# Dilated attention, dilation 16: the scores of all eight blocks in one list, both halves' transposes in one list, and the statistics three products earlier

## The chip, the cores and the metric

The kernel runs on one core of a Trainium2 chip. The metric is the device time of one launch in microseconds (us). TensorE (PE) multiplies matrices and loads its weights beside (PEld), VectorE (DVE) and ScalarE (ACT) do elementwise work, GpSimd (POOL) does little here, and SyncE (SP) issues nearly all DMAs. Each engine works through its own queue in order, and waits there for semaphores.

## The reference

Two layers: dilated sliding-window attention and an MLP, then a gated linear recurrence (HGRN) and an MLP, each with a residual and a layer norm. The change is in the attention: three head groups with (window, dilation) = (128, 1), (512, 4) and (2048, 16), 16 heads of 64, 1024 positions. Cut to what matters:

```python
def dilated_attention_mixer(x, w_in, w_out):
    proj = (x @ w_in).reshape(B, S, N_GROUPS, 3, ATTN_HEADS, ATTN_HEAD_DIM)
    for g, (window, dilation) in enumerate(DILATED_PATTERNS):
        q = rotary(proj[:, :, g, 0], pos)
        k = rotary(proj[:, :, g, 1], pos)
        o, lse = dilated_window_attention(q, k, proj[:, :, g, 2], window, dilation)
        ...
    wts = jax.nn.softmax(jnp.stack(lses, axis=0), axis=0)
    o = jnp.einsum('gbsh,gbshe->bshe', wts, jnp.stack(outs, axis=0).astype(F32))
    return o.reshape(B, S, ATTN_HEADS * ATTN_HEAD_DIM).astype(x.dtype) @ w_out
```

Inside `dilated_window_attention` every position attends to itself and to those at distances d, 2d, ... behind it: p = exp(s - m), l = sum p, o = (p / l) v, lse = m + log l.

## The kernel before

The attention takes its heads in eight pairs (`pr`). A pair and a dilation form a unit; the units go in the order dilation 16, 4, 1 within a pair (`GORD`), two units to a group (`a` = 0 and 1), twelve groups `gi`. The dilation-16 units are `a` = 0 of groups 0, 3, 6, 9 and `a` = 1 of groups 1, 4, 7, 10.

Each group's projection is 21 products (`product`): seven block products of a Strassen-like scheme (`ORDA`) for three columns of blocks (q, k, v). A product is twelve 128x512 matmuls, L832 to L834, with a weight tile `H` whose high half ScalarE writes (L499) and whose low half VectorE writes (L507), and operands `xh` and `xl` that SyncE loads (L461). Three PSUM banks hold the products.

What else the attention does is hung between the products. `fill[n]` is the list that runs after product n, then `low_w(n + 3)` and `split_w_(n + 5)` follow. TensorE and VectorE keep the order in which the code is written (`in_order`); a scheduler places ScalarE's and SyncE's instructions. `unit_work` gives a unit's steps, and tables say at which product after `base` they run: `ROPES` (rotation of q and k, with loads `rot` by SyncE, L539, used at L542 and L543), `UNIT0` and `OFFS` (six lists of `pieces`), `STATS` (three steps) and `MIX`.

For dilation 16 the lists of `pieces` hold: the scores of four blocks (`qk16`, L607), each followed by reductions on VectorE (L610: masked minimum of the negated scores, into `sS`) and exponentials on ScalarE (L614, with their sums); the transposes of v (`vtrans`, L557); the transposes of p (`ptr16`, L623); and the value products (`pv16`, L635).

The three steps of `STATS` come from `combine_tr`: TensorE transposes the units' minima and sums (L726) and ScalarE evicts them (`sr`); ScalarE's queue stores them to memory (L732); SyncE loads them back in another layout (`ml`, L739, eight DMAs for dilation 16). `ml` is a tile with one buffer, made anew for each pair. When the three units of a pair are done, `combine` (steps of `MIX`) turns `ml` into weights `fh` and `fl` on VectorE (L754 to L773, the last read of `ml` is `fl`, L773), SyncE brings them to `frow` (L778), TensorE spreads them (`fb`, L790), and VectorE multiplies the units' outputs by them (L793 to L796). After the last group, what is left of `fill` and the lists of the last pair are woven into the out-projection (L204 to L206, weights `woh`, `wol`, activations `aoh`, `aol`).

Of the kernel before, what the change touches and what calls it, by code (L numbers as in the profile page):

```python
# [9 lines left out]
F32 = mybir.dt.float32  # L10
F32R = mybir.dt.float32r
U8 = mybir.dt.uint8
AF = mybir.ActivationFunctionType
ALU = mybir.AluOpType
AX = mybir.AxisListType

P = 128
# [3 lines left out]
HD = 64  # L21
NPAIR = 8
DIL = (1, 4, 16)
# [46 lines left out]
def trunk_kernel(  # L70
# [24 lines left out]
    nc = tc.nc  # L95
    cp = ctx.enter_context(tc.tile_pool(name="cp", bufs=1))
    up = ctx.enter_context(tc.tile_pool(name="up", bufs=NSLOT))
    wp = ctx.enter_context(tc.tile_pool(name="wp", bufs=3))
# [7 lines left out]
    def bank(tag, name):  # L106
        return ps.tile([P, 512], F32, name=name, tag=tag, bufs={"mm": 3, "s": 2, "pt": 2, "o": 1}[tag])
# [4 lines left out]
    act = nc.scalar.activation  # L112
# [250 lines left out]
    def attention(pre, hc):  # L363
        out_of = []

        def evict(*args, **kw):
            act(*args, **kw)
            out_of.append(latest())
# [4 lines left out]
        groups = [units[i:i + 2] for i in range(0, len(units), 2)]  # L373
# [72 lines left out]
        def get_T(m, n):  # L446
            if m >= 7 * len(groups):
                return
            i = ORDA[m % 7]
            if m >= 7 and m % 7 < RESIDENT:  # L450
                opT[m] = opT[m % 7]
                return
            if m < 7:
                if m not in opT:
                    opT[m] = make_T(i)
                return
            if m not in opT:
                opT[m] = [None, None]
            opT[m][n] = [U("xhl"[0] + "hl"[n], F32R) for _ in range(2)]
            for q in range(2):  # L460
                nc.sync.dma_start(opT[m][n][q].bitcast(F32), xtd[i - 1, n][:, q * 1024:(q + 1) * 1024])  # L461
# [3 lines left out]
        def load_w(n):  # L465
            if n >= len(seq):
                return
            gi, i, j = seq[n]
            for half in {1: (0,), 2: (0,), 6: (0, 1), 7: (0, 1), 3: (0, 1), 5: (1,), 4: (1,)}[i]:
                if (gi, j, half) not in raw:  # L470
                    raw[gi, j, half] = U("w" + "ab"[half])
                    nc.sync.dma_start(raw[gi, j, half], w_attn[pairs[gi][j][half]])
# [36 lines left out]
        mask = cp.tile([P, 384], F32, name="mask")  # L509
# [35 lines left out]
        def pieces(pr, g, qT, kT, vT, og, sS, tail):  # L545
            st = {}
# [48 lines left out]
                            act(p[h], p[h], AF.Exp, bias=sS[:, 0, h, b:b + 1], scale=-1.0,  # L595
                                accum_out=sS[:, 1, h, b:b + 1])

            def qk16(j):
                sb = [bank("s", "s") for _ in range(2)]
                whole = wp.tile([P, 512], F32, name="p", tag="p")  # L600
                blocks = [(b, cl, slice((b % 4 * 2 + cl) * 64, (b % 4 * 2 + cl) * 64 + 64))
                          for b in range(4 * j, 4 * j + 4) for cl in range(2)]
                for b, cl, c in blocks:
                    q = slice(b * P + cl * 64, b * P + cl * 64 + 64)
                    for h in range(2):
                        r = slice(h * HD, (h + 1) * HD)
                        nc.tensor.matmul(sb[cl][(h ^ cl) * HD:(h ^ cl) * HD + HD, b % 4 * 64:b % 4 * 64 + 64],  # L607
                                         qT[r, q], kT[r, q], start=True, stop=True, skip_group_check=True)
                for b, cl, c in blocks:
                    nc.vector.tensor_tensor_reduce(whole[:, c], sb[cl][:, b % 4 * 64:b % 4 * 64 + 64],  # L610
                                                   mask[:, 320:384], -0.125, 3.0e38, op0=ALU.add, op1=ALU.min,
                                                   accum_out=sS[:, 0, cl, b:b + 1])
                for b, cl, c in blocks:
                    act(whole[:, c], whole[:, c], AF.Exp, bias=sS[:, 0, cl, b:b + 1], scale=-1.0,  # L614
                        accum_out=sS[:, 1, cl, b:b + 1])
                st["p", j] = whole

            def ptr16(j):
                pt = bank("pt", "ppt")
# [7 lines left out]
            def pv16():  # L627
                o = [bank(tag, "o") for tag in ("o", "pt")]
                for b in range(8):
                    pts = st["pt", b // 4]  # L630
                    for cl in range(2):
                        r = slice(cl * 64, cl * 64 + 64)
                        for h in range(2):
                            m = b % 4 * P + (h ^ cl) * 64
                            nc.tensor.matmul(o[cl][h * HD:(h + 1) * HD, b * 64:b * 64 + 64],  # L635
                                             st["vn"][r, b * P + h * HD:b * P + (h + 1) * HD], pts[r, m:m + 64],
                                             start=True, stop=True, skip_group_check=True)
                for cl in range(2):
                    evict(og.rearrange("p (n b x) -> p x b n", b=8, x=2)[:, cl],
                        o[cl].rearrange("p (b n) -> p b n", b=8), AF.Copy)  # L640

# [52 lines left out]
            def run(f, bs):  # L694
                return [lambda b=b: f(b) for b in bs]
# [10 lines left out]
                ]  # L706
            first, second = [lambda: pv(0, 1, 2, 3)], [lambda: pv(4, 5, 6, 7)]
            if g == 2:
                return [run(qk16, (0,)) + [vtrans], run(qk16, (1,)) + run(ptr16, (0,)), run(ptr16, (1,)),
                        [pv16], [], []]  # L710
            if g == 1:
                return [qks((0, 2), (4, 6)) + [vtrans], [shift] + qks((1,), (3,)) + run(ptr, ((0, 2), (4, 6))),
                        qks((5,), (7,)) + run(ptr, ((1,), (3,))), first + run(ptr, ((5,), (7,))), [], second]
# [95 lines left out]
        def at(slot, f):  # L809
            fill.setdefault(slot, []).append(f)  # L810
# [119 lines left out]
        for n in range(len(seq)):  # L930
            gi, i, j = seq[n]
            load_w(n + LOADW)
            if j == 0 and n // 3 < 6:
                get_T(n // 3 + 1, 1)
            if j == 1 and n // 3 >= 5:
                get_T(n // 3 + 2, 0)
            if j == 2 and n // 3 >= 5:
                get_T(n // 3 + 2, 1)
            if n == 11:
                constants()  # L940
            if n == 30:
                constants2()
            if n == 36:
                hc.append(hgrn_consts())
            if n == len(seq) - 2 * PREA - 3:
                early = pre(oN)
            if n >= len(seq) - 2 * PREA - 1:
                next(early, None)
            if n == FIRSTO[0]:
                acts.__enter__()  # L950
            if n == FIRSTO[1]:
                acts.__exit__()
            if n in KEEP:
                keep_T(KEEP[n])
            product(n)
            for f in fill.pop(n, []):
                f()
            if n in FIRSTW:
                for f, m in FIRSTW[n]:
                    (split_w_, low_w, third_a, third_b, third_c, third_d)[f](m)  # L960
            else:
                low_w(n + SPLITW - 2)
                split_w_(n + SPLITW)
            if n % 21 == 14:
                last = gi == len(groups) - 1
                base = n + 7
                work = [unit_work(gi, a, base) for a in range(2)]
                for a in range(2):
                    adds, rope_of, core, stats, mix = work[a]
                    steps = [f for t in range(2) for f in (lambda rope_of=rope_of, t=t: rope_of(t),  # L970
                                                           lambda adds=adds, t=t: adds[t][0](),
                                                           lambda adds=adds, t=t: adds[t][1]())]
                    if last:
                        both = [lambda f=f: (f[0](), f[1]()) for f in (steps[1:3], steps[4:6])]
                        tail.append(([steps[0], both[0], steps[3], both[1]], core, stats, mix))
                        continue
                    for k, f in zip(ROPES[a], steps):
                        at(base + k, f)
                    for k, f in enumerate(core):
                        at(base + UNIT0 + OFFS[a][k], f)  # L980
                    for k, f in zip(STATS[a], stats):
                        at(base + k, f)
                    for k, f in zip(MIX[a], mix):
                        at(base + k, f)
                if last:
                    for a in range(2):
                        for k, f in list(zip(ROPES0[a], tail[a][0])):
                            if k < -1:
                                at(base + k, f)
                                tail[a][0].remove(f)  # L990
# [957 lines left out]
    pr = Out(w_attn_out, "a", 0)  # L1948
    hc = []
    oN, fill = attention(pr.pre_steps, hc)  # L1950
    gw = GateW()
    f = ffn(0, x1d, ln_ffn_g[0], ln_ffn_b[0], False, (gw.ask, lambda: gw.prefetch(0)))
# [6 lines left out]
    f = ffn(1, x5d, ln_ffn_g[1], ln_ffn_b[1], True)  # L1959
# [81 lines left out]
```

## Time and profile before

| what | us |
|---|---|
| median of 3 runs | 2724.91 (2723.44 to 2725.13) |
| the profiled execution | 2721.81 |
| its span, first to last instruction | 2720.0 |
| attention's units, first to last list | about 85 to 960 |
| out-projection beside the last units | from about 890 |

The granted TensorE clock of that execution was 0.999. Timeline rows give the start, the length, the engine, the line, the operation, the tile written and the tiles read, and the count; idle time before an instruction and what ended it stand in brackets. TensorE's starts tell more than its lengths, since matmuls overlap. Of dilation 16, TensorE's records count two to a matmul in the scores and the value products.

### The profile page before, as it was taken

What the parts mean: (1) busy time and instruction counts of PE and PEld (TensorE: products, weight loads), DVE (VectorE), ACT (ScalarE), POOL (GpSimd) and SP (SyncE); (2) the same over time, 40 slices, a digit from 0 to 9 for tenths busy, and PEclk for the clock granted to TensorE, in tenths of its full rate; (3) what the DMA queues carried; (4) which work ended last, traced back from release to release, by engine and by line L of the source; (5) the groups of instructions that cost most, each with busy time, mean ns of one, the idle gap of its engine ahead of it and who ended that gap; (6) DMA issues with size and microseconds to landing.
All of it is one profiled execution on the core that took longest, in us unless ns stands there. A gap on an engine that the chain in (4) does not pass through costs nothing.

```text
span 2720.0 us, 44143 instructions
## 1 busy us (share of the span) xinstructions
PE 2694.8 (99%) x16256; PEld 2199.3 (81%) x16256; DVE 2042.1 (75%) x3887; ACT 1385.0 (51%) x3044; POOL 39.2 (1%) x44
## 2 busy tenths in 40 slices
PE   9999999999999999999999999999999999999998
PEld 7787888888788677888888888788878888888887
DVE  8868877787887788876687686656478886678687
ACT  5555555555565455444544345555453544545443
POOL 0000000000000002000000000000000100000000
PEclk9999999999999999999999999999999999999999
DMA  8877666766767443554665652010233464485653
GB/s 303 269 226 226 219 217 203 246 216 220 251 208 245 126 137 140 200 187 151 229 238 189 206 170 93 32 63 32 74 128 116 150 225 161 154 305 174 224 178 124
DMA packets 208152, 493.66 MB, mean 181 GB/s; under 512 B 30016, under 2 KB 44864, under 8 KB 207936
## 3 DMA queue, kind: packets, MB, share of 16 engines
q1 hardware_dynamic: 204384, 481.14, 53.0%
q0 software_dynamic: 2304, 8.39, 0.8%
q8 instruction: 128, 2.10, 0.3%
q10 hardware_dynamic: 1248, 1.31, 0.2%
q14 instruction: 88, 0.72, 0.1%
HBM read 362.69 MB, written 94.11 MB: 168 GB/s over the span
## 4 chain that ended last, share of the span: by engine, by line
PE 92%; DVE 5%; ACT 1%; issue 1%; DMA 0%; POOL 0%; SPq 0%; DVEq 0%; ACTq 0%; POOLq 0%
PE pmm L834 7%; PE pmm L832 7%; PE pmm L833 7%; PE pup L1357 7%; PE pup L1355 7%; PE pup L1356 7%; PE pdy L1510 4%; PE pdy L1509 4%; PE pdy L1506 4%; PE pmm L192 3%; PE pdx L1509 3%; PE pdx L1510 3%; PE pdx L1506 3%; PE pmm L194 3%; PE pmm L193 3%; PE pmm L205 2%
## 5 line engine op out<-in xcount | busy, mean ns | idle before, releaser
L832 PE MATMUL pmm<-xh,H 128*128 128x512 f32 x1008 | 404.1, 401 | 1.4 <-ACT H L499 1.4
L834 PE MATMUL pmm<-xh,H 128*128 128x512 f32 x1008 | 395.6, 392 | 2.2 <-DVE H L507 2.1
L833 PE MATMUL pmm<-xl,H 128*128 128x512 f32 x1008 | 393.3, 390 | 0.7 <-DVE xl L158 0.7
L834 PEld LDWEIGHTS pmm<-xh,H 128*128 128x128 f32 x1008 | 189.5, 188 | 46.7 <-DVE H L507 5.4
L832 PEld LDWEIGHTS pmm<-xh,H 128*128 128x128 f32 x1008 | 189.9, 188 | 39.6 <-ACT H L499 2.2
L833 PEld LDWEIGHTS pmm<-xl,H 128*128 128x128 f32 x1008 | 190.1, 189 | 37.8 <-DVE xl L158 1.1
L1506 PE MATMUL pdy<-dT,dS 128*128 128x512 f32 x512 | 199.2, 389 | 0.0
L1509 PE MATMUL pdy<-dT,dS 128*128 128x512 f32 x512 | 199.2, 389 | 0.0
L1510 PE MATMUL pdy<-dT,dS 128*128 128x512 f32 x512 | 199.2, 389 | 0.0
L157 ACT ACTIVATE dS<-dr 128x512 fp32r<-128x512 f32 x192 | 119.3, 622 | 67.5 <-PE pdy L1510 36.1
L192 PE MATMUL pmm<-f0nh,wh 128*128 128x512 f32 x384 | 153.3, 399 | 0.0
L193 PE MATMUL pmm<-f0nl,wh 128*128 128x512 f32 x384 | 149.8, 390 | 0.0
L194 PE MATMUL pmm<-f0nh,wl 128*128 128x512 f32 x384 | 149.8, 390 | 0.0
L595 ACT ACTIVATE p<-p,stats 128x192 f32<-128x192 f32 (+1 forms) x256 | 108.8, 428 | 62.4 <-DVE stats L592 62.2
L158 DVE TENSOR_TENSOR dS<-dr,dS 128x512 fp32r<-128x512 f32 x192 | 131.4, 685 | 9.2 <-ACT dS L157 9.2
L157 ACT ACTIVATE dT<-hold 128x512 fp32r<-128x512 f32 x128 | 80.1, 626 | 80.8 <-DVE hold L1485 33.4
L1316 ACT ACTIVATE H<-wc 128x512 fp32r<-128x512 f32 x128 | 77.2, 625 | 76.6 <-DVE wc L1309 46.3
L1506 PEld LDWEIGHTS pdy<-dT,dS 128*128 128x128 f32 x512 | 96.1, 188 | 20.0
L1509 PEld LDWEIGHTS pdy<-dT,dS 128*128 128x128 f32 x512 | 96.1, 188 | 20.0
L1510 PEld LDWEIGHTS pdy<-dT,dS 128*128 128x128 f32 x512 | 96.1, 188 | 19.9
L592 DVE CUSTOM_DVE_ANT_0 p<-s,mask 128x192 f32<-128x192 f32 (+1 forms) x256 | 71.1, 337 | 45.3 <-PE s L579 32.4
L499 ACT ACTIVATE H<-wc 128x512 fp32r<-128x512 f32 x108 | 66.6, 629 | 75.6 <-DVE wc L491 73.5
(426 smaller groups left out, 6881.9 us busy)
## 6 DMA issues: line engine op xcount, KB each, us to landing
xh<-xtd SPq DMA_DIRECT2D x110, 512.0 KB
xl<-xtd SPq DMA_DIRECT2D x110, 512.0 KB
dr<-hd SPq DMA_DIRECT2D x192, 256.0 KB
dr<-in_w_down_dram SPq DMA_DIRECT2D x128, 256.0 KB
rot<-e SPq DMA_DIRECT2D x192, 128.0 KB
wa<-in_w_up_dram SPq DMA_DIRECT2D x48, 512.0 KB
wb<-in_w_attn_dram SPq DMA_DIRECT2D x36, 512.0 KB
wa<-in_w_attn_dram SPq DMA_DIRECT2D x33, 512.0 KB
```

Source lines behind the costliest of these rows:

```text
L157: act(hi, raw, AF.Copy)
L192: nc.tensor.matmul(o, wh[:, k], xs.h(k), start=k == 0, stop=False)
L193: nc.tensor.matmul(o, wh[:, k], xs.l(k), start=False, stop=False)
L194: nc.tensor.matmul(o, wl[:, k], xs.h(k), start=False, stop=k == NK - 1)
L832: nc.tensor.matmul(o, wh, hi[k // 2][:, c], start=begin and k == 0, stop=False, skip_group_check=True)
L833: nc.tensor.matmul(o, wh, lo[k // 2][:, c], start=False, stop=False, skip_group_check=True)
L834: nc.tensor.matmul(o, wl, hi[k // 2][:, c], start=False, stop=end and k == 3, skip_group_check=True)
L1355: nc.tensor.matmul(o, wh, xf.h(b, k), start=begin and k == 0, stop=False, skip_group_check=True)
L1356: nc.tensor.matmul(o, wh, xf.l(b, k), start=False, stop=False, skip_group_check=True)
L1506: nc.tensor.matmul(o[q], h, T_[:, L], start=begin, stop=False, skip_group_check=True)
L1509: nc.tensor.matmul(o[q], h, T_[:, R], start=False, stop=False, skip_group_check=True)
L1510: nc.tensor.matmul(o[q], l, T_[:, L], start=False, stop=end, skip_group_check=True)
```

## The change

`qk16` now makes the scores of all eight blocks in one call: 32 matmuls into two PSUM banks of which it uses all columns (it used half), with two p tiles. The reductions and exponentials follow in two halves. The lists of dilation 16 become: scores and v's transposes; nothing; the transposes of both halves; the value products; nothing; nothing. The value products keep their list, the fourth. Their two evictions change places. The three `STATS` steps of dilation-16 units run three products earlier (9, 10, 12 and 19, 20, 22). Nothing is computed differently.

```diff
-            def qk16(j):
+            def qk16():
                 sb = [bank("s", "s") for _ in range(2)]
-                whole = wp.tile([P, 512], F32, name="p", tag="p")
+                whole = [wp.tile([P, 512], F32, name="p", tag="p") for _ in range(2)]
...
-                for b, cl, c in blocks:
-                    nc.vector.tensor_tensor_reduce(whole[:, c], sb[cl][:, b % 4 * 64:b % 4 * 64 + 64],
...
+                for half in (blocks[:8], blocks[8:]):
+                    for b, cl, p in half:
+                        nc.vector.tensor_tensor_reduce(p, sb[cl][:, b * 64:b * 64 + 64], mask[:, 320:384], -0.125, 3.0e38,
+                                                       op0=ALU.add, op1=ALU.min, accum_out=sS[:, 0, cl, b:b + 1])
+                    for b, cl, p in half:
+                        act(p, p, AF.Exp, bias=sS[:, 0, cl, b:b + 1], scale=-1.0, accum_out=sS[:, 1, cl, b:b + 1])
...
-                for cl in range(2):
+                for cl in (1, 0):
                     evict(og.rearrange("p (n b x) -> p x b n", b=8, x=2)[:, cl],
...
-                return [run(qk16, (0,)) + [vtrans], run(qk16, (1,)) + run(ptr16, (0,)), run(ptr16, (1,)),
-                        [pv16], [], []]
+                return [[qk16, vtrans], [], run(ptr16, (0, 1)), [pv16], [], []]
...
-                        at(base + k, f)
+                        at(base + k - (3 if DIL[groups[gi][a][1]] == 16 else 0), f)
```

The lines after the change are two or three lower from the transposes on: L607 stays, L611 are the reductions, L622 p's transposes, L634 the value products, L724 the statistics' transpose, L737 the load of `ml`, L776 that of `frow`, L788 `fb`, L830 to L832 the products.

TensorE in the first dilation-16 unit, before (the matmuls of the products between the lists are left out):

```order
L834 MATMUL pmm<-xh,H 128x512
L607 MATMUL s<-kT,qT 64x64 x16
L557 MATMUL vpt<-ident,vT 128x128 x8
...
L607 MATMUL s<-kT,qT 64x64 x16
L623 MATMUL ppt<-ident,p 128x128 x4
L832 MATMUL pmm<-xh,H 128x512
...
L623 MATMUL ppt<-ident,p 128x128 x4
...
L635 MATMUL o<-pts,vn 64x64 x32
```

The same place after the change:

```order
L832 MATMUL pmm<-xh,H 128x512
L607 MATMUL s<-kT,qT 64x64 x32
L557 MATMUL vpt<-ident,vT 128x128 x8
...
L622 MATMUL ppt<-ident,p 128x128 x8
...
L724 MATMUL mpt<-ident,stats 128x128
...
L634 MATMUL o<-pts,vn 64x64 x32
```

Four interruptions of the products became three, the statistics' transpose moved ahead of the value products, and these stayed.

SyncE's queue in the second group (`a` = 1 is a dilation-16 unit; `frow`'s loads belong to the pair before, `ml`'s to the new pair), before:

```order
L778 DMA frow<-fh 2x8x128
L461 DMA xl<-xtd 128x1024 x2
L778 DMA frow<-fh 2x8x128 x2
L461 DMA xh<-xtd 128x1024 x2
L778 DMA frow<-fl 2x8x128 x3
L739 DMA ml<-mdram 8x8x8 x8
L461 DMA xl<-xtd 128x1024 x2
L539 DMA rot<-e 32x1024 x4
```

The same place after the change:

```order
L776 DMA frow<-fh 2x8x128
L461 DMA xl<-xtd 128x1024 x2
L776 DMA frow<-fh 2x8x128
L737 DMA ml<-mdram 8x8x8 x8
L461 DMA xh<-xtd 128x1024 x2
L776 DMA frow<-fh 2x8x128
L776 DMA frow<-fl 2x8x128 x3
L461 DMA xl<-xtd 128x1024 x2
L539 DMA rot<-e 32x1024 x4
```

The eight loads of `ml` now stand ahead of one load of `fh`, a pair of `xh` loads and the three loads of `fl`.

TensorE where the last pair's lists are woven into the out-projection (`fb` spreads the weights of the pair before the last; L579 are scores, L648 transposes, L677 value products of the last units), before:

```order
L206 MATMUL pmm<-woh,aol 128x512
L677 MATMUL o<-pts,vn 64x128
L790 MATMUL fb<-frow,bsel 128x512
...
L648 MATMUL ppt<-ident,p 128x128 x6
L204 MATMUL pmm<-woh,aoh 128x512
L579 MATMUL s<-kT,qT 64x192 x8
L790 MATMUL fb<-frow,bsel 128x512
L648 MATMUL ppt<-ident,p 128x128 x2
```

The same place after the change:

```order
L205 MATMUL pmm<-wol,aoh 128x512
L788 MATMUL fb<-frow,bsel 128x512
L647 MATMUL ppt<-ident,p 128x128 x2
L206 MATMUL pmm<-woh,aol 128x512
L647 MATMUL ppt<-ident,p 128x128 x3
L788 MATMUL fb<-frow,bsel 128x512
L579 MATMUL s<-kT,qT 64x192 x8
L647 MATMUL ppt<-ident,p 128x128 x5
L676 MATMUL o<-pts,vn 64x128
L788 MATMUL fb<-frow,bsel 128x512
```

The three `fb` of the first half now stand within nine rows, where other steps and out-projection matmuls stood between them; out-projection matmuls that stood among the last scores now stand ahead of this place or behind it.

More of the change, by code (lines that the diff above doesn't have):

```diff
@@ L596, in qk @@
                                 accum_out=sS[:, 1, h, b:b + 1])
-            def qk16(j):
+            def qk16():
                 sb = [bank("s", "s") for _ in range(2)]
-                whole = wp.tile([P, 512], F32, name="p", tag="p")
-                blocks = [(b, cl, slice((b % 4 * 2 + cl) * 64, (b % 4 * 2 + cl) * 64 + 64))
-                          for b in range(4 * j, 4 * j + 4) for cl in range(2)]
-                for b, cl, c in blocks:
+                whole = [wp.tile([P, 512], F32, name="p", tag="p") for _ in range(2)]
+                blocks = [(b, cl, whole[b // 4][:, (b % 4 * 2 + cl) * 64:(b % 4 * 2 + cl) * 64 + 64])
+                          for b in range(8) for cl in range(2)]
+                for b, cl, _ in blocks:
                     q = slice(b * P + cl * 64, b * P + cl * 64 + 64)
@@ L606, in qk16 @@
                         r = slice(h * HD, (h + 1) * HD)
-                        nc.tensor.matmul(sb[cl][(h ^ cl) * HD:(h ^ cl) * HD + HD, b % 4 * 64:b % 4 * 64 + 64],
+                        nc.tensor.matmul(sb[cl][(h ^ cl) * HD:(h ^ cl) * HD + HD, b * 64:b * 64 + 64],
                                          qT[r, q], kT[r, q], start=True, stop=True, skip_group_check=True)
[L609 to L616, printed above, removed]
+                for half in (blocks[:8], blocks[8:]):
[4 more added lines that the diff above has]
+                        act(p, p, AF.Exp, bias=sS[:, 0, cl, b:b + 1], scale=-1.0, accum_out=sS[:, 1, cl, b:b + 1])
+                st["p", 0], st["p", 1] = whole
             def ptr16(j):
```

## The prediction

> **What bounds the kernel now.** I read the page first, for the busiest engine and the chain that ended last, then busy time by stretch for the attention (85 to 1070 us), then what TensorE waited for there, and last the timelines around single units. In order: the page, the stretches (PE, PEld, DVE, ACT, POOL busy, granted clock, DMA share, GB/s) and the waits.
>
> ```profile
> PE 2694.8 (99%) x16256; PEld 2199.3 (81%) x16256; DVE 2042.1 (75%) x3887; ACT 1385.0 (51%) x3044; POOL 39.2 (1%) x44
> ...
> PE 92%; DVE 5%; ACT 1%; issue 1%; DMA 0%; POOL 0%; SPq 0%; DVEq 0%; ACTq 0%; POOLq 0%
> ```
> ```profile
> 85.00:255.00 170.00, 168.92 (x1347) 135.90 (x1340) 132.88 (x338) 97.19 (x286) 0.95 (x1) 1.00 0.71 223
> ...
> 890.00:1000.00 110.00, 105.34 (x776) 78.93 (x775) 82.02 (x189) 51.97 (x154) 0.00 (x0) 1.00 0.41 124
> ```
> ```profile
> PE ppt L623 <- ACT p L614: 0.6, 2, 0.3
> ```
>
> TensorE sets the time: 99% busy, 92% of the chain, clock 1.00. Between 85 and 255 us it idles 1.08 us in all; between 890 and 1000, where the attention's last pairs run beside the out-projection, 4.66 us. A change that moves work can gain only three things: breaks in the stream of 128x512 matmuls, the few waits of this unit, and something in the tail. What it can lose is anything that makes a 99% busy engine wait.
>
> **A, one break fewer in TensorE's stream.** The first of eight dilation-16 units, before (start, length, engine, line):
>
> ```profile
> 84.70 0.69 PE L607 MATMUL s<-kT,qT 64*64 64x64 f32 x32
> 85.32 1.09 PE L557 MATMUL vpt<-ident,vT 128*128 128x128 f32 x8
> ...
> 91.51 0.39 PE L834 MATMUL pmm<-xh,H 128*128 128x512 f32 x1
> 91.83 0.69 PE L607 MATMUL s<-kT,qT 64*64 64x64 f32 x32
> 92.46 0.66 PE L623 MATMUL ppt<-ident,p 128*128 128x128 f32 x4
> 92.87 0.48 PE L832 MATMUL pmm<-xh,H 128*128 128x512 f32 x1
> 93.18 0.39 PE L833 MATMUL pmm<-xl,H 128*128 128x512 f32 x1
> 93.41 0.39 PE L834 MATMUL pmm<-xh,H 128*128 128x512 f32 x1
> ```
>
> Matmuls inside a product start 0.23 us apart (93.18 to 93.41). The second list cost 91.51 to 92.87 = 1.36 instead of 0.23, and the next matmul came 0.31 after instead of 0.23: 1.21 us are removed. Its second half of the scores goes behind the first half and adds 0.62 (84.70 to 85.32); its four transposes go behind the other four and add 0.41 (92.46 to 92.87). Net -0.18 a unit. If scores that follow scores run at the pitch of the 64 records of the value products, 1.10 us for 64 or 0.55 for 32, it is -0.25:
>
> ```profile
> 105.46 1.16 PE L635 MATMUL o<-pts,vn 64*64 64x64 f32 x64
> 106.56 0.50 PE L832 MATMUL pmm<-xh,H 128*128 128x512 f32 x1
> ```
>
> Eight units: **-1.4 to -2.0**; I take -1.7. The value products stay in the fourth list, so nothing is gained there; the swapped evictions cost the same two instructions.
>
> **B, the transposes no longer wait for the last exponentials.**
>
> ```profile
> 98.43 0.38 PE L623 MATMUL ppt<-ident,p 128*128 128x128 f32 x2
> ...
> 99.81 0.47 PE L832 MATMUL pmm<-xh,H 128*128 128x512 f32 x1
> ```
> ```profile
> 891.72 0.49 PE L623 MATMUL ppt<-ident,p 128*128 128x128 f32 x3
> ...
> 892.54 0.48 PE L832 MATMUL pmm<-xh,H 128*128 128x512 f32 x1
> ...
> 896.63 0.50 PE L834 MATMUL pmm<-xh,H 128*128 128x512 f32 x1 [0.51 <-DVE H L507]
> ```
>
> The waits view gave 0.6 us in two waits; with what a stop costs around it, these four transposes take 98.43 to 99.81 = 1.38 in the first unit, against 0.41 unhindered: -0.97. In the last it is 0.82 against 0.41, but four us later TensorE waits for VectorE's H all the same, so 0 to -0.41 is kept. I take **-1.0** together. What is late next? Sixteen reductions now stand in a row on VectorE and sixteen exponentials on ScalarE:
>
> ```profile
> 88.89 0.21 DVE L610 CUSTOM_DVE_ANT_0 p<-s,mask 128x64 f32<-128x64 f32 x1
> ...
> 90.04 0.69 DVE L507 TENSOR_TENSOR H<-wc,H 128x512 fp32r<-128x512 f32 x1
> ```
> ```profile
> 89.15 0.35 ACT L614 ACTIVATE p<-p,stats 128x64 f32<-128x64 f32 x1
> ...
> 91.82 1.05 ACT L367 ACTIVATE vn<-vpt 128x512 f32<-128x512 f32 x2
> ```
>
> Eight reductions take 1.15 us (88.89 to 90.04), eight exponentials 2.67. The H written at 90.04 would be ready at 91.88 in place of 90.73; TensorE reads it at 93.41. ScalarE gets to its next work at 94.5 in place of 91.82, and all sixteen exponentials are done then, four us ahead of the transposes at 98.43. Banks freed by its evictions are asked for three products (8.2 us) later. So I cost this at nothing; if that cover failed, it would be up to 1.15 us (one run of reductions) in each unit, 9 us in all, for which no row of these units speaks.
>
> **C, the earlier statistics block SyncE's queue.** The statistics come back through memory into the tile `ml`, of which there is one buffer. The eight loads of `ml` now stand three products earlier in SyncE's queue, ahead of loads that they followed, and wait there until VectorE has read the previous pair's `ml` (L773). Before, in the second group:
>
> ```profile
> 226.49 1.30 SPq L778 DMA_DIRECT2D frow<-fh  x2
> 227.90 0.81 SPq L461 DMA_DIRECT2D xh<-xtd  x2
> 233.37 1.95 SPq L778 DMA_DIRECT2D frow<-fl  x3
> 235.43 2.80 SPq L739 DMA_DIRECT2D ml<-mdram  x8
> ...
> 239.25 2.46 SPq L539 DMA_DIRECT2D rot<-e  x4
> ```
> ```profile
> 232.81 0.54 DVE L773 TENSOR_TENSOR fl<-ml,fh 16x384 fp32r<-16x384 f32 x1
> ```
>
> SyncE already stops from 228.71 until 233.37 for `fl`. Now `ml` is what it stops at, and behind it stand one load of `fh` (half of 1.30), and the `xh` pair (0.81): ml 233.4 to 236.2, then 0.65 and 0.81 and 1.95, so `rot` is issued at 239.25 + 1.5 us with the gaps between. Who waits for `rot`:
>
> ```profile
> 248.93 1.23 DVE L542 TENSOR_TENSOR rot<-rot,sinT 128x1024 f32<-128x1024 f32 x1 [3.44 <-DMA rot<-e]
> ...
> 251.33 0.69 DVE L507 TENSOR_TENSOR H<-wb,H 128x512 fp32r<-128x512 f32 x1
> ```
> ```profile
> 251.64 0.39 PE L833 MATMUL pmm<-xl,H 128*128 128x512 f32 x1
> 252.07 0.50 PE L834 MATMUL pmm<-xh,H 128*128 128x512 f32 x1
> ```
> ```profile
> 477.02 0.68 DVE L507 TENSOR_TENSOR H<-wb,H 128x512 fp32r<-128x512 f32 x1
> ```
> ```profile
> 479.33 0.39 PE L834 MATMUL pmm<-xh,H 128*128 128x512 f32 x1
> ```
> ```profile
> 705.13 0.69 DVE L507 TENSOR_TENSOR H<-wb,H 128x512 fp32r<-128x512 f32 x1
> ```
> ```profile
> 706.57 0.39 PE L834 MATMUL pmm<-xh,H 128*128 128x512 f32 x1
> ```
>
> VectorE stood idle 3.44 us for that `rot`, and H came 2.4 us after; TensorE's matmul at 252.07 already came 0.20 late. H is done 1.63 us ahead of its matmul in the fifth group (477.70, 479.33) and 0.75 ahead in the eighth (705.82, 706.57). If `rot` lands 1.5 later, TensorE stops 1.5, 0 and 0.75 there: **+2.3**. The lower bound is 0: data may land no later than now, since the queue is empty while SyncE waits and `rot` now competes with one load pair less. A gain is out of reach, since `rot` is nowhere issued earlier. The upper bound is about +4, for a shift of 2.2 (2.2, 0.6, 1.4). In groups 4, 7 and 10 the same rule moves loads behind the wait, but nothing there waits for `rot`; I cost them at 0.
>
> A sentence of the Trainium skill bears on this (DMA: Bandwidth & Descriptors, "Anatomy of one DMA — SWDGE (gpsimd) path"): a DMA's wait for a semaphore is served on the issuing sequencer, before dispatch, not in the DMA engines. The trace agrees for SyncE's queue: nothing is issued between 228.71 and 233.37. By this rule the sum has C in it (-0.4); were the wait served behind the queue, it would be without it (-2.7).
>
> **D, the tail.** The last unit's statistics now run inside the product loop, and the lists that are woven into the out-projection move up by two entries. The stretch where scores, exponentials and value products of the last pair alternate:
>
> ```profile
> 943.00:967.00 24.00, 23.79 (x293) 16.54 (x291) 14.56 (x54) 18.23 (x58) 0.00 (x0) 1.00 0.40 132
> ```
> ```profile
> 943.00:967.00 24.00, 1.75 (x4) 0.76 (x4) 1.00 0.40 132
> ```
>
> The second row is one of the three out-projection lines there (L204; L205 and L206 have four each too). Twelve matmuls at 0.23, 2.8 us, fill TensorE between the steps; in the new order up to ten of them stand ahead of this stretch. Their 2.3 us are the most that this can cost, if nothing else fills the places; against it, the last pairs' work up to 916 may end up to 1.1 us earlier, since eight reductions leave VectorE's dense phase. ScalarE, 18.23 of 24 us, hides most of neither. I take **0**, from -1.5 to +2.3.
>
> **Sum:** -1.7 - 1.0 + 2.3 + 0 = -0.4 us. The profiled execution took 2721.81 us (its span 2720.0), so 2721.4 on its own basis. It lies 3.1 under the median of the runs shown, 2724.91; on that basis I say 2724.5.
>
> **Rivals.** (1) The wait on SyncE is hidden: C is 0, and the kernel gains 2.7; 2722.2. For it speaks that DMA engines idle while SyncE waits; against it, that VectorE waits for `rot` now. With the tail's best, -1.5 and the rest of A, it comes to -4.5, and only with more in the tail than I can show past 5.4. (2) Slower: the blocked SyncE queue starves TensorE in six groups and not two. The place is the `ml` load ahead of `xl`, `xh` and `rot`; the price is the shift less the slack, and it decides where a load lands more than about 1.6 us later, the largest slack above. `xh` and, in groups 4, 7 and 10, the weights' loads shift by 8 to 10 us; if the three groups with `rot` lose 2.2, 0.6 and 1.4 and the three others 1.5 each, it is +8.7 - 2.7 = +6.0: 2731. For it speaks that DMA share is 0.71 with loads asked in bursts; against, that of TensorE's waits between 85 and 890 us none is put down to a load: both entries of that view, the one above and a second like it, name ScalarE. (3) The tail loses its cover: +2.3 on the forecast, 2726.8. (4) The change does not do what it says: only the break counts (the value products did not move), and C and D come to nothing; -1.7, 2723.2.
>
> **Chances.** About 0.2% (5.4 us) is what a measurement of this kernel can tell from no change. Forecast 0.37; rival 1 as priced 0.15; rival 3 0.11; rival 4 0.08: all within 5.4. Rival 2 0.15, of which 0.02 stay within. That leaves 0.14 for rival 1 with more found in the tail than the 1.5 that I can show, which ends faster by over 5.4. So faster 0.14, same 0.73, slower 0.13. The range reaches from -6.0 (A, B and the tail at their best, 4.5, and 1.5 more in the tail) to +5.1 (beyond the worst ends of A, C and D, +3.9, and most of the way to rival 2): 2718.9 to 2730.0.
>
> **What would show it.** A: in a unit, a product follows the second list 0.23 us after the last one, and scores take some 1.2 us before the transposes of v. B: no transposes of p wait for exponentials. C: `ml` stands ahead of `fl` in SyncE's queue; `rot` issued near 240.8; VectorE's wait for it near 5 us and a stop of TensorE near 252. D: idle time of TensorE between 890 and 1000 against 4.66. I am wrong if H or a bank is late in units where no row shows a wait now, or if the later layers start otherwise.

## The result, and the profile after

The changed kernel takes 2732.24 us (median of 15 runs, 2726.89 to 2735.52), the kernel before 2723.62 (15 runs on the same chips, 2721.30 to 2725.13). The ratio is 1.0030, 95% interval 1.0022 to 1.0038: 8.6 us slower, where no change was forecast and the range ended at 2730.0. The profiled execution took 2729.22 us, its span is 2727.5 us.

Busy time in the two stretches of the attention that were shown of before (PE, PEld, DVE, ACT, POOL, clock, DMA share, GB/s):

```profile
85.00:255.00 170.00, 166.10 (x1335) 134.35 (x1333) 129.84 (x326) 94.70 (x277) 0.96 (x1) 1.00 0.68 216
...
890.00:1000.00 110.00, 103.65 (x770) 76.71 (x769) 79.25 (x174) 48.90 (x131) 0.00 (x0) 1.00 0.41 123
```

TensorE idles 3.90 us in the first, where it idled 1.08, and 6.35 in the second, where it idled 4.66; the clock is the same. The view of waits, TensorE's from 85 to 890 us of the changed kernel, says for whom:

```profile
PE ppt L647 <- ACT vn L367: 4.6, 4, 2.9
PE pmm L832 <- DVE H L507: 3.1, 3, 1.5
```

Neither line is about the units that were rewritten. The waits for the exponentials (0.6 us) are gone, as forecast; 3.1 us for H are new, and one wait of 2.9 for vn. The same view from 890 to 1150 us has a longest wait for the layer norm (2.7, where it was 1.2) and two for pts that were not there:

```profile
PE lnpt L253 <- DVE fs L336: 2.7, 1, 2.7
...
PE ppt L647 <- ACT pts L367: 0.6, 2, 0.4
```

The longer wait for the layer norm is no loss of its own. In the kernel before, TensorE stops 1.7 us shortly ahead of it for an `H` of the MLP, and that stop has shrunk to 0.3; both stops together are 2.9 us in both traces. Before:

```profile
PE pup L1357 <- DVE H L1324: 1.7, 1, 1.7
PE lnpt L253 <- DVE fs L336: 1.2, 1, 1.2
```

The rewritten unit itself does what was worked out, and the first one shows it on TensorE's timeline:

```profile
85.73 1.16 PE L607 MATMUL s<-kT,qT 64*64 64x64 f32 x64
...
86.82 1.09 PE L557 MATMUL vpt<-ident,vT 128*128 128x128 f32 x8
...
98.50 0.39 PE L832 MATMUL pmm<-xh,H 128*128 128x512 f32 x1
98.73 1.04 PE L622 MATMUL ppt<-ident,p 128*128 128x128 f32 x8
99.53 0.48 PE L830 MATMUL pmm<-xh,H 128*128 128x512 f32 x1
```

All scores run in one piece, 1.09 us (85.73 to 86.82); the eight transposes take 0.80 us (98.73 to 99.53) and wait for nothing.

Where the loss arises, read off the starts of the same product in both traces: the changed kernel falls behind by 3.0 us in one step at product 38, by 1.4, 0.4 and 1.7 us at products 74, 137 and 200, and by 3.5 us between product 251 and the end; of these, 2.6 are lost by the last matmul of the out-projection, ahead of the MLP. The first dilation-16 unit gains 1.3 us, the next six 0.38 each and the last 0.6. The losses are the three places that the experiments take apart.

**Product 38, ScalarE.** First the changed kernel, then two rows of before:

```profile
122.08 0.20 ACT L1676 ACTIVATE hc_e<-hc_e 128x16 f32<-128x16 f32 x1
...
127.21 0.21 ACT L1718 ACTIVATE hc_low<-hc_low 128x8 f32<-128x8 f32 x1 [2.36 <-DVE hc_C L1717]
127.33 1.03 ACT L367 ACTIVATE vT<-pmm 128x512 f32<-128x512 f32 x1
128.16 1.11 ACT L367 ACTIVATE vn<-vpt 128x512 f32<-128x512 f32 x2
```
```profile
122.50 1.06 ACT L367 ACTIVATE vT<-pmm 128x512 f32<-128x512 f32 x1
123.36 1.11 ACT L367 ACTIVATE vn<-vpt 128x512 f32<-128x512 f32 x2
```
```profile
128.83 0.44 PE L647 MATMUL ppt<-ident,p 128*128 128x128 f32 x2 [2.92 <-ACT vn L367]
```

ScalarE evicted vT and vn at 122.5 before. Now the activations of the HGRN constants (`hc`, which a later layer needs) stand ahead of them in its queue, and `hc_low` ends a chain of small operations on VectorE. vn comes 4.8 us later, and TensorE stops for 2.92. The first of these activations (`hc_e`) stood ahead of vT before the change too; the other three (two `Ln`, `hc_A` and `hc_C`, and `hc_low`) are new there.

**Product 74, SyncE, VectorE, TensorE**, the place of step C:

```profile
229.34 0.63 SPq L776 DMA_DIRECT2D frow<-fh  x1
236.23 2.75 SPq L737 DMA_DIRECT2D ml<-mdram  x8
239.03 0.82 SPq L461 DMA_DIRECT2D xh<-xtd  x2
239.89 0.64 SPq L776 DMA_DIRECT2D frow<-fh  x1
240.57 1.92 SPq L776 DMA_DIRECT2D frow<-fl  x3
242.59 0.82 SPq L461 DMA_DIRECT2D xl<-xtd  x2
243.50 2.57 SPq L539 DMA_DIRECT2D rot<-e  x4
```
```profile
235.63 0.54 DVE L771 TENSOR_TENSOR fl<-ml,fh 16x384 fp32r<-16x384 f32 x1
...
253.19 1.23 DVE L542 TENSOR_TENSOR rot<-rot,sinT 128x1024 f32<-128x1024 f32 x1 [4.88 <-DMA rot<-e]
...
255.59 0.68 DVE L507 TENSOR_TENSOR H<-wb,H 128x512 fp32r<-128x512 f32 x1
```
```profile
256.33 0.50 PE L832 MATMUL pmm<-xh,H 128*128 128x512 f32 x1 [1.49 <-DVE H L507]
```

SyncE issues nothing from 229.97 to 236.23, when VectorE has done with the old `ml` (L771, the row at 235.63); then `ml`, the `xh` pair, `fh` and `fl` go out, and `rot` at 243.50. At this point the changed kernel is 2.83 us behind (product 70), so `rot` comes 243.50 - 239.25 - 2.83 = 1.42 later than before. VectorE waits 4.88 for it (3.44 before), and TensorE 1.49 for the H behind it.

### The profile page after: what moved, and what is told of

It is laid out like the page before. It is cut to its first block, busy times and chain, and to the rows that moved or that the text cites. A ratio compares the mean times of both kernels' runs of the same rounds, so it can differ in the third digit from the quotient of the medians.

```text
span 2727.5 us, 44121 instructions
## 1 busy us (share of the span) xinstructions
PE 2692.8 (99%) x16256; PEld 2198.0 (81%) x16256; DVE 2043.5 (75%) x3887; ACT 1384.4 (51%) x3044; POOL 39.8 (1%) x44
## 4 chain that ended last, share of the span: by engine, by line
PE 89%; DVE 5%; DMA 2%; issue 2%; ACT 1%; SPq 1%; POOL 0%; DVEq 0%; ACTq 0%; POOLq 0%
PE pup L1355 7%; PE pup L1353 7%; PE pup L1354 7%; PE pmm L832 7%; PE pmm L830 7%; PE pmm L831 7%; PE pdy L1507 4%; PE pdy L1508 4%; PE pdy L1504 4%; PE pmm L192 3%; PE pdx L1507 3%; PE pdx L1508 3%; PE pdx L1504 3%; PE pmm L194 3%; PE pmm L193 3%; PE pmm L204 2%
## 5 line engine op out<-in xcount | busy, mean ns | idle before, releaser
L830 PE MATMUL pmm<-xh,H 128*128 128x512 f32 x1008 | 403.3, 400 | 1.8 <-ACT H L499 1.0
L832 PE MATMUL pmm<-xh,H 128*128 128x512 f32 x1008 | 394.9, 392 | 6.5 <-DVE H L507 6.3
L832 PEld LDWEIGHTS pmm<-xh,H 128*128 128x128 f32 x1008 | 189.3, 188 | 51.6 <-DVE H L507 11.0
L830 PEld LDWEIGHTS pmm<-xh,H 128*128 128x128 f32 x1008 | 189.5, 188 | 40.8 <-ACT H L499 1.9
L367 ACT ACTIVATE e<-pmm 128x512 f32<-128x512 f32 x96 | 56.8, 593 | 91.1 <-PE pmm L832 90.8
```

The lines of the kernel that those rows point to most:

```text
L830: nc.tensor.matmul(o, wh, hi[k // 2][:, c], start=begin and k == 0, stop=False, skip_group_check=True)
L832: nc.tensor.matmul(o, wl, hi[k // 2][:, c], start=False, stop=end and k == 3, skip_group_check=True)
```

## The experiments

Every run was timed with the kernel before on the same chip; differences of medians below are against those runs. Theory A: three separate costs, all from the earlier statistics, and a gain from the lists. Its rivals: the long rows of reductions and exponentials (B), and what each run names.

**The lists alone.**

```diff
-                        at(base + k - (3 if DIL[groups[gi][a][1]] == 16 else 0), f)
+                        at(base + k, f)
```

> The change without the earlier statistics (STATS as before), so the lists alone. Theory A (three separate costs, all of them from the earlier statistics: ScalarE's order at the HGRN constants +3.0, loads behind ml in SyncE's queue +3.5, the tail +3.4; the lists themselves gain 4.2): 4 us faster than before, about 2719.5; no wait of TensorE at 128.8, 256.3, 484 or 711 us beyond those of before, each later dilation-16 unit 0.35 us shorter. Theory B (the sixteen reductions and exponentials in a row make H and evictions late): the waits stay, and the time is 4 to 8 us above before.

Measured: 2719.27 us against 2722.63, ratio 0.9986 (0.9977 to 0.9995): 3.4 us faster than before, and faster than both kernels. TensorE's waits from 85 to 890 us:

```profile
PE ppt L647 <- ACT vn L367: 1.3, 3, 0.5
PE pmm L832 <- DVE H L507: 0.4, 2, 0.2
```

Theory B falls: with the same sixteen reductions and exponentials in a row there is no stop worth the name, and all of the loss is in the earlier statistics. The gain in the trace is the 4.2 us that was expected (1.4, six times 0.38, and 0.6 in the eight units).

**The statistics alone** (the kernel before with the other line of the diff).

```diff
-                        at(base + k, f)
+                        at(base + k - (3 if DIL[groups[gi][a][1]] == 16 else 0), f)
```

> Before with the earlier statistics alone, lists as before. Theory A: all three losses and no gain, 3.0 + 4 to 6 + 2 to 3.5: 9 to 12 us slower than before, 2732 to 2735; waits at 128 us and at products 73, 136 and 199. Theory B (the lists bring the loss): the same as before.

Measured: 2735.60 against 2723.18, 12.4 us slower, a little over the expected end. The waits stand where the changed kernel has them (vn 2.9; H three times over 0.9). The parts add up, to within what different chips and few runs allow: 12.4 for the statistics, less 3.4 for the lists, against 8.6 for both.

**The middle alone: early statistics in groups 1, 4 and 7**, added to the lists.

```diff
+                        at(base + k - (3 if DIL[groups[gi][a][1]] == 16 and gi in (1, 4, 7) else 0), f)
```

> The lists, with the earlier statistics in groups 1, 4 and 7 alone: SyncE's queue blocked by ml as in the changed kernel, tail and HGRN constants as in the lists alone. Theory A: waits of TensorE for H of 1.4, 0.4 and 1.7 us at products 73, 136 and 199 and no others; 3.5 us slower than the lists alone, 0.7 us faster than before. Theory D (the loads behind ml cost nothing, other things made H late): the same as the lists alone.

Measured: 2724.10 against 2722.63, so 4.8 us slower than the lists alone (-3.4). The waits for H in its trace:

```profile
PE pmm L832 <- DVE H L507: 4.4, 4, 2.1
```

These are 2.1, 1.1 and 0.8 us at the three products, and 0.3 at 98.6 us, ahead of all early statistics: the same three places, in other sizes than in the changed kernel (waits of 1.5 and 1.4 at the first and the third, and 0.4 by the starts at the second). By the starts of the products this run loses 3.6, 1.4 and 1.1 us there. The traced execution was the slowest of the run (2728.76 us), and its first place holds more than the wait: see the last section. Theory D falls.

**The tail alone: early statistics in the last unit.**

```diff
+                        at(base + k - (3 if DIL[groups[gi][a][1]] == 16 and gi == 10 else 0), f)
```

> The lists, with the earlier statistics in the last dilation-16 unit (group 10) alone: the tail as in the changed kernel, the rest as in the lists alone. Theory A: 3.4 us slower than the lists alone, all of it behind product 251; about 0.8 us faster than before. Theory C (the tail's loss comes from arriving later and not from its order): the same as the lists alone.

Measured: 2721.15 against 2722.63, 1.9 us slower than the lists alone, where 3.4 was expected. The order of the tail has a price. The expected size, from one pair of traces, was too large: it took in 0.9 us that the changed kernel loses in the MLP behind the out-projection, and the lists alone lose 1.1 us there too. Up to the last matmul of the out-projection this run loses 2.5 us against before, the changed kernel 2.6 and the lists alone 0.1.

**The HGRN constants after product 39.**

```diff
-            if n == 36:
+            if n == 39:
                 hc.append(hgrn_consts())
```

> The changed kernel with the HGRN constants made after product 39 and not 36, which puts their activations behind the eviction of vT and vn in ScalarE's queue; nothing else moves on TensorE. Theory A: the wait of 2.9 us for vn at 128.8 us goes, the others stay: 3 us faster than the changed kernel. Theory B: the wait stays, because vn is late for the long run of exponentials, and the time is that of the changed kernel.

Measured: 2734.38 against 2722.63, 11.8 us slower: worse than the changed kernel, against theory A. ScalarE and TensorE:

```profile
124.58 0.46 ACT L595 ACTIVATE p<-p,stats 128x192 f32<-128x192 f32 x1 [3.66 <-DVE stats L592]
...
125.03 0.44 ACT L595 ACTIVATE p<-p,stats 128x192 f32<-128x192 f32 x1
...
125.47 1.00 ACT L367 ACTIVATE vT<-pmm 128x512 f32<-128x512 f32 x1
```
```profile
126.95 0.44 PE L647 MATMUL ppt<-ident,p 128*128 128x128 f32 x2 [2.83 <-ACT vn L367]
```

The constants are gone from here, and vT is still late: now two exponentials of the next scores stand ahead of it, and they wait 3.66 us for VectorE. So it need not be the constants; vT's place behind whatever waits for VectorE could be the cause, or something that holds vT itself. The next run decides that. The run is slower than the changed kernel because it loses another 4.2 us between products 40 and 45, beside the constants' new place, where TensorE stops 1.49 us for `p`.

**vT ahead, by a forced order on ScalarE alone.** Instructions on TensorE, VectorE and SyncE stand as in the changed kernel.

```diff
-                hc.append(hgrn_consts())
+                hc.append(hgrn_consts([out_of[-1].name]))
...
             act(t, t, AF.Ln)
+            behind(latest(), then)
...
         act(low, low, AF.Exp, scale=-1.0)
+        behind(latest(), then)
```

> The changed kernel with one order forced on ScalarE: the three logarithms and exponentials of the HGRN constants that follow the first stand behind the evictions of vT and vn (as they stood before the change), all other engines as in the changed kernel. Moving the constants to a later product did not remove the wait at 127 us, since other instructions that wait for VectorE (two exponentials) then stood ahead of vT. Theory A (what costs 3 us there is the place of vT and vn in ScalarE's queue): no wait for vn at 128 us, 3 us faster than the changed kernel. Theory B (vT could not be evicted earlier, a DMA or a bank holds it): the wait stays.

Measured: 2727.32 against 2723.18, 4.1 slower than before where the changed kernel is 8.6 slower: 4.5 us recovered, by medians from different chips whose ratios have intervals that touch (1.0005 to 1.0022 here, 1.0022 to 1.0038 there). ScalarE:

```profile
120.34 0.61 ACT L499 ACTIVATE H<-wc 128x512 fp32r<-128x512 f32 x1
120.86 1.06 ACT L367 ACTIVATE vT<-pmm 128x512 f32<-128x512 f32 x1
121.72 1.10 ACT L367 ACTIVATE vn<-vpt 128x512 f32<-128x512 f32 x2
```

vT goes right behind the instruction ahead of it, nothing holds it, and the wait for vn at 128 us is gone. What costs there is the place in ScalarE's queue.

**Only the loads of `ml` late**, at their old product in the first seven units; transposes, evictions and stores stay early. TensorE's and VectorE's orders are word for word those of the changed kernel.

```diff
+                    for i_, (k, f) in enumerate(zip(STATS[a], stats)):
+                        at(base + k - (3 if DIL[groups[gi][a][1]] == 16 and (i_ < 2 or gi == 10) else 0), f)
```

> As the run with all loads of ml late, except in the last unit (group 10), whose load stays early: TensorE and VectorE have exactly the order of the changed kernel, only SyncE and ScalarE differ. Theory A: the waits at 128 us and at products 73, 136 and 199 go, the tail's loss of about 2 us stays: 7 us faster than the changed kernel, 1.5 us faster than before. Theory E: most of the changed kernel's loss stays, since TensorE's and VectorE's orders do.

Measured: 2722.87 against 2723.18, 0.3 faster than before and 8.9 better than the changed kernel, more than expected. SyncE's queue at the place shown above:

```profile
233.05 1.96 SPq L776 DMA_DIRECT2D frow<-fl  x3
235.12 2.81 SPq L737 DMA_DIRECT2D ml<-mdram  x8
238.02 0.82 SPq L461 DMA_DIRECT2D xl<-xtd  x2
238.93 2.47 SPq L539 DMA_DIRECT2D rot<-e  x4
```

`fl` is again ahead of `ml`, and `rot` goes out at 238.93. All waits for H at the three products are gone, and so is the stop at 128 us: with the load late, vT stands ahead of the constants in ScalarE's queue. Both losses hang on where the loads of `ml` stand in SyncE's queue. The first is a wait in that queue; the second comes through the order that the scheduler gives ScalarE. By what reckoning it moves vT was not tried. Nor was the first unit's load moved by itself; that it is this one is argued from its place near product 38, and from there being no such stop in the runs with early statistics in groups 1, 4 and 7 or 10 alone.

**All loads late, the last unit's too.**

```diff
+                        at(base + k - (3 if DIL[groups[gi][a][1]] == 16 and i_ < 2 else 0), f)
```

> The lists and the earlier statistics, but their third step, the loads of ml, at its old product in all eight units. Theory A (transposes, evictions and stores three products earlier cost nothing, only the loads' place in SyncE's queue does): as the lists alone, 3.4 us faster than before, with no waits for H at products 73, 136 and 199. Theory E (the statistics' transpose and eviction ahead of the value products hold TensorE or ScalarE): slower than the lists alone by more than 1 us in units that no load touches.

Measured: 2722.06 against 2723.18, 1.1 faster than before, where 3.4 was expected. No wait for H in the loop, but the tail is not as in the lists alone: two of the three steps of the last unit still run inside the loop, and the lists behind it still move up. The expectation had overlooked that.

**The tail's lists put back in step**, by two empty entries where the two steps stood.

```diff
+        for n in (254, 256):
+            at(n, lambda: None)
         done = [f for n in sorted(fill) for f in fill[n]]
```

With the early statistics in the last unit alone:

> As the run with the earlier statistics in the last unit alone, but with two empty entries put where its two steps stood in what is left of the lists after the last product, so that the other entries meet the same out-projection matmuls as before the change; the steps themselves stay early. Theory F (the tail's loss is that its lists are two entries out of place): as the lists alone, 3.4 us faster than before and 1.9 faster than the run without empty entries; TensorE's waits for pts and for the layer norm as before. Theory G (the early steps themselves cost it): the same as the run without empty entries, 1.5 us faster than before.

Measured: 2720.68 against 2723.95, 3.3 faster than before; the lists alone were 3.4 faster, the same without empty entries 1.5. With the loads of `ml` late and all else early:

> The changed kernel with the loads of ml at their old product in the first seven units and the two empty entries in the tail. Theory A with F: all three losses gone though lists, transposes, evictions and stores are those of the change: 3.4 us faster than before, about 2719.5, the same as the lists alone. Theory E (the early steps have a price of their own in the loop): 1 us or more slower than the lists alone.

Measured: 2721.28 against 2723.95, 2.7 faster, where the lists alone gave 3.4; the intervals (0.9983 to 1.0001 here) overlap. The run without the empty entries was 0.3 faster. In the traces the waits for pts are gone in both, but there is a new wait in the tail, here in the first of the two:

```profile
PE mpt L721 <- DVE og L791: 0.9, 1, 0.9
```

Up to the last matmul of the out-projection these two runs lose 1.1 and 1.2 us against before, where 2.4 to 2.6 are lost without the empty entries and 0.1 by the lists alone. So putting the lists back in step recovers over half of the tail's loss. By the medians it could be all of it; by the traces some 1 us stays. It is not settled whether that is the early steps or the order: `in_order` ends with the product loop, and TensorE's rows between about 938 and 980 us still differ from those of the lists alone, though the lists are in step. The run with all loads late loses only 1.4 us there with its lists out of step, so the place of the last unit's load has a part in it too.

## Why the prediction was wrong

The sign of the pieces was mostly right, and the sum was not: forecast -0.4, measured +8.6. The step that failed is the reckoning of what the earlier loads touch. The sum let them delay `rot` alone (C, +2.3) and put nothing for ScalarE's order and 0 for the tail; the runs showed +4.8, +4.5 and +1.9 there.

- **A and B** (forecast -1.7 and -1.0) had the right sign and mechanism: the lists alone gave -3.4 in the medians and -4.2 in the eight units of the trace. B was sized well: the first and the last unit gain 1.2 us more than the others. A was too small: a unit gains 0.38 us and not 0.18 to 0.25, in the main since the second half of the scores adds 0.47 behind the first (1.09 for all of them, 0.62 for half), not 0.62 or 0.55; the transposes add the 0.4 that was taken.
- **"So I cost this at nothing"**, the sixteen reductions and exponentials in a row: right. The lists alone show no wait from it.
- **C** (forecast +2.3, range 0 to 4) had the right mechanism and a size too small: +4.8 in the run of the middle alone, beyond the upper bound of about 4. The issue of `rot` moved by 1.42 (forecast 1.5), VectorE's wait became 4.88 (forecast near 5) and the first stop 1.49 (forecast 1.5). The other two stops are what was mis-sized: 0 and 0.75 were taken, 0.4 and 1.7 came in the changed kernel, and about 1.4 and 1.1 in the run of the middle alone (where the first place cost 3.6). `rot` was issued 1.4 later there too, but what VectorE does with it began 1.9 and 2.2 later (480.09 and 708.22 us against 474.61 and 702.73, less the 3.6 and 3.3 that the kernel was behind): the working took the shift of the issue for that of the landing, and the landing varies. VectorE's wait at the fifth group was 1.66 before, 3.54 in the changed kernel and 4.50 in the run of the middle alone, in this order:

```profile
474.61 1.23 DVE L542 TENSOR_TENSOR rot<-rot,sinT 128x1024 f32<-128x1024 f32 x1 [1.66 <-DMA rot<-e]
...
702.73 1.23 DVE L542 TENSOR_TENSOR rot<-rot,sinT 128x1024 f32<-128x1024 f32 x1 [2.54 <-DMA rot<-e]
```
```profile
480.09 1.23 DVE L542 TENSOR_TENSOR rot<-rot,sinT 128x1024 f32<-128x1024 f32 x1 [3.54 <-DMA rot<-e]
...
708.22 1.22 DVE L542 TENSOR_TENSOR rot<-rot,sinT 128x1024 f32<-128x1024 f32 x1 [4.77 <-DMA rot<-e]
```
```profile
482.18 1.23 DVE L542 TENSOR_TENSOR rot<-rot,sinT 128x1024 f32<-128x1024 f32 x1 [4.50 <-DMA rot<-e]
```

- **The step that was missing**: the prediction looked for "groups 4, 7 and 10" and for what waits for `rot`, and costed a late eviction nowhere. That the load of the first unit's statistics would also change ScalarE's order, and put vT behind activations that wait for VectorE, was in none of the terms and in no rival. It costs 3.0 us in the profiled execution and 4.5 in the medians. The new order could have been read before the run: in ScalarE's queue three of the constants' activations stood ahead of vT.
- **D** (forecast 0, from -1.5 to +2.3): the taken value was wrong, the upper bound right: +1.9 in the medians. Cover was lost as rival 3 said, with waits for pts that were not there before, between 943 and 970 us; the hoped-for earlier end of VectorE's phase did not come (TensorE's wait for H near 900 us is 1.0 in the changed kernel, 0.5 before).
- **Rival 2** (slower) gave 2731, by a queue that starves TensorE in six groups. It ended near the measured time for another reason: three groups lose, not six, and the rest is vT and the tail; that it came close is luck. Rival 1, a hidden wait on SyncE, falls: TensorE loses time at all three places. Its support was misread as well. The DMA engines do not idle while SyncE stops from 228.71 to 233.37: in the trace of before their share is 0.85 from 230 to 232 us and 0.63 from 232 to 234. It is low (0.1 to 0.3) only from 234 to 240, and from 240 to 254, after `rot` is issued, it is 1.0 or more.

In medians: -3.4 for the lists, +4.5 for vT's place, +4.8 for the blocked queue and +1.9 for the tail make +7.8, against 8.6 measured; the four come from different chips, and the second is the least certain.

## What to carry to other kernels

A step that is moved takes its DMA with it: a load of a single-buffered tile that must wait for its last reader stops every load behind it in the same queue, so move the computation early and leave the load where its wait is already over. After a change of order, read the queues of all engines, those that are never the bound too: two evictions behind an instruction that waits cost here as much as the change gained. Lists that are paired by position go out of step when an entry leaves them; an empty entry in its place keeps the pairing, though not the order that a scheduler then makes of it.

## What was not expected of the hardware

The first microseconds differ from execution to execution though the programs are the same there: product 3 starts at 14.95 us in the trace of before and 3.71 us later in that of the middle alone, where TensorE waited for the first operand:

```profile
9.58 0.50 PE L830 MATMUL pmm<-xh,H 128*128 128x512 f32 x1 [1.53 <-ACT xh L157]
```

Half clock adds to this: the granted clock was 0.50 from 11.3 to 14.8 us in the trace of the middle alone, and from 37.1 to 40.5 in that of before, where the changed kernel's trace has none. By product 21 the traces lie from 0.8 us ahead of before to 2.7 behind it. A single pair of spans is therefore no measure of an effect of 2 us; the starts of the same product on either side of a place are.

A stop of TensorE can cost more than its own length. Around the stop at product 74 in the trace of the middle alone TensorE was busy 1.32 of 3.41 us, and for the next 3.41 us its granted clock was 0.50; matmuls there start 0.43 us apart (257.24 to 257.67) and not 0.23, and the place costs 3.6 us for a wait of 2.1. The columns are again PE, PEld, DVE, ACT, POOL, clock, DMA share and GB/s:

```profile
253.69:257.10 3.41, 1.32 (x6) 1.01 (x6) 3.38 (x9) 0.33 (x1) 0.00 (x0) 1.00 1.00 351
257.10:260.51 3.41, 3.41 (x21) 2.37 (x21) 3.38 (x9) 3.41 (x12) 0.00 (x0) 0.50 1.03 285
```

In the traces a stretch of half clock is 3.41 us long, and where a trace has several they start a whole number of 3.41 us apart (35 and 268 of them with the constants after product 39). Divide the ten traces that have such a stretch, from 8 us on, into pieces of 3.41 us that start where the stretches do. A piece in which TensorE idled for 1.7 us or more was followed by one at 0.50 in all eleven cases, and a piece with less than 1.5 never was; between the two both happened. So it matters how a stop falls on the pieces. The stop of 2.9 us at product 38, in the trace of the statistics alone, lay across two of them, and the clock stayed at 1.00:

```profile
124.10:127.51 3.41, 1.76 (x21) 0.96 (x19) 2.92 (x20) 0.54 (x3) 0.00 (x0) 1.00 0.01 2
127.51:130.93 3.42, 2.13 (x13) 1.86 (x14) 3.27 (x13) 3.42 (x7) 0.00 (x0) 1.00 0.17 37
```

The changed kernel's trace has no half clock between its first and its last products, and it is 3.0 us below the median of its runs. Five of those 15 runs have a mean granted clock of 0.997; the runs of before that list a clock have 0.998 or 0.999. This may be why vT's place costs more in the medians than in the trace, and why the changed kernel's runs spread over 8.6 us, those of before over 3.8 and those of the lists alone over 2.4; it is argued and not shown. The three stops for H also have other sizes in each trace, and whether the two are all of the spread stays open.
